# Context rows and key rotations placed behind weight splits, chain buffers turned by one, weight sums three steps later

## The chip, the cores and the metric

The kernel runs on one core of a Trainium2 chip, in fp32 throughout. The metric is the device time of one execution in microseconds. The engines of the core are named as the profile names them: PE (TensorE) multiplies matrices, DVE (VectorE) and ACT (ScalarE) work on elements, POOL (GpSimd) and SP (SyncE) here mostly issue transfers (DMAs). Each engine works through its own instructions in the order in which the program lists them, and waits at an instruction until what that instruction needs is there.

## The reference

One layer of a diffusion block over 512 latent tokens (width 2048) and 256 context tokens. What matters for the change:

```python
shift, scale, gate = jnp.split(silu_c @ w_ada[l] + b_ada[l], 3, axis=-1)
shift_c, scale_c, gate_c = jnp.split(silu_cc @ w_ada[l] + b_ada[l], 3, axis=-1)
h = _modulate(_rmsnorm(xs, norm_g[l]), shift[:, None], scale[:, None])
hc = _modulate(_rmsnorm(cs, norm_g[l]), shift_c, scale_c)
pc_kv = hc @ w_l[:, OFF_K:OFF_ZA]          # keys and values of the context
p = h @ w_l                                # 512 x 2048 times 2048 x 9216
k = _rope(_rmsnorm(_heads(p, OFF_K, N_KV_HEADS), k_norm_g[l]), cos, sin)
...
y_a = (attn * jax.nn.silu(z_a)) @ w_pa
y_b = (_fourier_mix(u_b) * jax.nn.silu(z_b)) @ w_pb
y = (g_a * y_a + g_b * y_b) @ w_o
return _rmsnorm(xs + gate[:, None] * y, final_g)
```

## The kernel before

Every large product is done in fp32 from three reduced-precision matmuls (`mm3`): each operand is split into a high part (`whi`, written by ACT, L176) and the rest (`wlo`, written by DVE, L177), and hi·hi, hi·lo and lo·hi are added in PSUM. Each split of 128x1024 weights thus takes one ACT and one DVE instruction. A *piece* of weights is 128x1024 numbers (512 KB); the 512-token matrix products use it in 12 matmuls of 512 columns.

On top of that stands a Winograd-like scheme with seven products for eight (`PRODUCTS`: P1, Q5, P2, Q6, P7, Q3, Q4). A *group* is one 1024-column block of a weight matrix: seven products of four pieces each, 28 pieces, 336 matmuls. Groups 0 to 7 make the input projection (5, called KV, makes keys and values, and with them the context's, by a second set of matmuls on each piece); then come 48 steps of attention; then groups 10 and 11 (branch projections, three pieces to a product) and groups 8 and 9 (output projection, four pieces).

Four of the seven products use sums of weight blocks that are built up one after the other in the four *chain buffers* `R0` to `R3` (R_1303 to R_1306): a product with `stage` 0 loads its first block into chain buffer `pc` from SP (L215), the later stages add another block to it, by a POOL transfer that accumulates (L280) or by DVE (L259). A chain buffer is loaded for the next group only when its last stage has been split (`left[pc]`). Up to four pieces are split ahead of the one that PE is at (`look`).

Raw weights come through four to six buffers (`raw_pools`), loaded by SP (L212) as soon as a split or an add has read the earlier contents. So DVE's reading sets when SP may issue, and SP issues in the program's order.

Parts that share the engines with the weight splits in the stretch of groups 3 to 5:

- `context_row(i, raw)` (L1070), called four times, forms the seven operand forms of a quarter of the context in one buffer `cparts` (part of the tile `qr`): four weightings on DVE (L1077), a subtraction (L1080), six adds (L1086), four ACT instructions (L1089, L1090), and then a DMA that ACT issues, `cf_d[i]` (L1091). There is only one such buffer, so the weightings of row i+1 wait until the write of row i has landed. Group 5 loads `cf_d` again as pieces `("cf", name)`.
- `load_rotations` (L928; its transfers L929 and L930 are issued by ACT) loads the cos/sin tables and the key gains into the same tile `qr` ahead of group 5, and `rotations` (L935) multiplies them by two DVE instructions. They are used when the first products of keys are done, at the end of P2 of group 5.

In attention, `filler()` fits in the products of the FNet branch (pieces `("pab", j, pc)`, loaded by SP from `in_w_pab`, split by ACT and DVE in order with the softmax work). `weight_sum(n)` (L1410) builds six sums of weight blocks for P7 of groups 10 and 11: a POOL load (L1415), an accumulating POOL load (L1416) and a POOL write to `p7_d` (L1417), at three steps in a row, from step 10 on. Chain buffers 0 to 2 hold gates at that time (`load_gb`, L1216), chain buffer 3 is a scratch tile of `values` (L1315, L1316).

What sets the order: the program is emitted in the order of the code, and a scheduler then moves instructions within each engine by its own estimate of their due times; `tc.issue_after(x)` forces the instructions in its block behind instruction x in that order, without a wait at run time for another engine. `last_split[-1][1]` is the DVE instruction of the weight split that was emitted last, which is up to four pieces ahead of PE.

Of the kernel before, what the change touches and what calls it, by code (L numbers as in the profile page):

```python
# [13 lines left out]
ALU = mybir.AluOpType  # L14
# [76 lines left out]
CHUNKS = (0, 2, 1, 3)  # L91
BRANCH_A, BRANCH_B = 10, (6, 7)
A_CHUNKS = ((0, 2), (1, 3))
A_FORM = {p[0]: (p[1],) for p in PRODUCTS} | {"Q4": ("A12", "A22"), "P2": ()}


# [23 lines left out]
def block_kernel(ctx, tc, xT, ctx_rows, ctx_toks, x, c_row, w_ss, w_gate, vecs, qkg, rope, dft_c, dft_s,  # L120
                 w_start, w_g, w_pab, w_o, final_g, out):
    nc = tc.nc
# [20 lines left out]
    p7_d = dsc.tile([2, 3, P, 1024], F32, name="p7_d")  # L143
# [37 lines left out]
    chain, left = [], [0] * 4  # L181
# [12 lines left out]
    def stream(key, src, *a, **k):  # L194
        todo.append(Piece(key, src if isinstance(src, list) else [src], *a, **k))
# [183 lines left out]
    def stream_product(name, g, w, by_dve, pieces=4):  # L379

        what = next(p[2] for p in PRODUCTS if p[0] == name)
        for pc in range(pieces):
            key = (name, g, pc)
            part = lambda i: w[CHAIN[i][0], CHAIN[i][1], pc]
            if isinstance(what, tuple) and name == "P7" and g >= BRANCH_A:
                stream(key, [p7_d[g - BRANCH_A, pc]], 1024, 2, pc=pc)
            elif isinstance(what, tuple):
                off = name == "P7"
                stream(key, [w[a, b, pc] for a, b in what], 1024, 2, pc=pc, nxt=part(3) if off else None, off=off)
            else:  # L390
                stream(key, [part(what)] if what in by_dve else [], 1024, 2, stage=what, pc=pc,
                       nxt=part(what + 1) if what < (3 if g >= BRANCH_A else 2) and what + 1 not in by_dve else None)
                todo[-1].first = part(0)

# [674 lines left out]

    def context_row(i, raw):  # L1070

        t, raw = cparts, raw.rearrange("p (b s c) -> p b s c", b=4, s=2)
        a11, a21, a12, a22, s3, s2, s4 = (t[:, f] for f in range(7))
        for j in range(2):
            for q in range(2):
                kb = 2 * i + j + 8 * q
                nc.vector.scalar_tensor_tensor(t[:, 2 * q : 2 * q + 2, j, :], raw[:, 2 * q + j], gain[:, kb, 1:2],  # L1077
                                               crs.rearrange("p (s c) -> p s c", s=2), op0=ALU.mult, op1=ALU.mult)

        nc.vector.tensor_tensor(s3, a11, a21, op=ALU.subtract)  # L1080
        for j in range(2):
            sa, sb = (shift[:, 2 * i + j + 8 * q, 1:2] for q in range(2))
            d = sums[:, 6 + j : 7 + j]
            nc.vector.tensor_tensor(d, sa, sb, op=ALU.subtract)
            for o, x, c, y, op in ((s2, a22, sb, s3, ALU.add), (s4, a12, sb, s2, ALU.subtract), (a21, a21, d, a22, ALU.subtract)):
                nc.vector.scalar_tensor_tensor(o[:, j], x[:, j], c, y[:, j], op0=ALU.add, op1=op)  # L1086
        for j in range(2):
            sa, sb = (shift[:, 2 * i + j + 8 * q, 1:2] for q in range(2))
            nc.scalar.activation(a11[:, j], a11[:, j], ACT.Identity, bias=sa)  # L1089
            nc.scalar.activation(t[:, 2:4, j, :], t[:, 2:4, j, :], ACT.Identity, bias=sb)  # L1090
        nc.scalar.dma_start(cf_d[i], t)  # L1091
# [49 lines left out]
    for g, kind in enumerate(KINDS):  # L1141
        if g == 3:
            jobs += [lambda: None] * 12 + [context_norm, lambda: None, lambda: None, context_spread]
        elif g == KV:
            while jobs:
                job()
            assert not any(p[2] == "raw1" for e in ahead for p, _ in e.raws)
        elif g == KV + 1:
            qzs.close()
            gvs, gvp = region("gvp", "right", reuse_waits="tile")  # L1150
            hl_pools += range(MORE_HL)
        group = Group(g, forms, new_ev, {"qz": qz_done, "kv": kv_done, "gate": gate_done}[kind], {"a": "x", "b": "y", "c": "x"})
        if g == KV:
            group.more = Context()
        for name in ONE_GROUP:
            if (g, name) in ((0, "Q4"), (KV + 1, "P1")):
                assert not any(p[2] == "raw0" for e in ahead for p, _ in e.raws)
                load_row(int(g > 0))
            elif (g, name) == (1, "Q5"):
                silu_of_row(0, flat(new_ev()))  # L1160
            if (g, name) == (0, "P7"):
                raw_pools.remove((rp, 1, "raw0", 1))
            if (g, name) == (0, "Q5"):
                hl_pools += range(MORE_HL)
            elif (g, name) == (0, "P2"):

                with tc.issue_after(last_split[-1][1].ins):
                    rotations(HD ** -0.5)
            elif (g, name) == (KV, "P1"):
                load_rotations(qkg[:, 2:4, :])  # L1170
            elif (g, name) == (KV, "Q5"):
                rotations(1.0)
            elif (g, name) == (KV - 1, "Q3"):
                raw_pools.remove((rp, 1, "raw1", 1))
                hl_pools[:] = [p for p in hl_pools if not isinstance(p, int)]
            elif (g, name) == (KV + 1, "Q6"):
                raw_pools += [(rp, 1, "raw1", 1), (gvp, 2, "raw", 2)]
            elif (g, name) == (LAST, "P7"):
                raw_pools.remove((gvp, 2, "raw", 2))
            elif (g, name) == (LAST, "Q3"):  # L1180

                free += [(fms[i], f"s{i}") for i in (4, 5, 6, 7, 12, 13, 14, 15, 8, 9, 10, 11, 2, 3, 0, 1)]
                for h in range(2):
                    load_head(h)
            elif (g, name) == (LAST, "Q4"):
                hl_pools[:] = [p for p in hl_pools if not isinstance(p, int)]
                get_keys(0)
                jobs.append(lambda: turn_queries(0, pair("y")[:, 0, :]))
            group.run(name)
# [16 lines left out]
    assert not any(p[0] is gvp for e in ahead for p, _ in e.raws)  # L1206
    todo_gb, gb = [(j, h) for j in CHUNKS for h in range(2)], {}

    left[:3] = [1] * 3

    def load_gb():
        if todo_gb:
# [212 lines left out]
    for i in range(NSTEP + 3):  # L1425
        h, t = divmod(i, 4)
        if i < NSTEP:
            if t == 2 and h + 2 < NH:
                load_head(h + 2)
            if i % 12 == 10 and i // 12 + 1 < NKV:  # L1430
                get_keys(i // 12 + 1)
            scores(i)
        want = min(3 + 61 * (i + 1) // NSTEP, 64) + (i == NSTEP - 1)
        if want > filled:
            fill(1)
            filled += 1
        if i % 2 == 0 and i >= 4:
            values((i - 4) // 2)
        if 1 <= i <= NSTEP:
            turn(i - 1)  # L1440
            divide(i - 1)
        if t == 1 and h + 1 < NH:
            turn_queries(h + 1, b1())
        if want > filled:
            fill(want - filled)
            filled = want
        if 10 <= i < 28:
            n, step = divmod(i - 10, 3)
            if step == 0:
                weight_sum(n)  # L1450
            else:
                summed[-1][step]()
            if step == 2:
                give(summed.pop()[0])
        if i == 3:
            with tc.issue_after(maxima[0].ins), tc.issue_after(maxima[1].ins):
                e = take((1024,))
                silu_of_row(1, e)
                give(e)
        if i == 33:  # L1460
            for p in more_raw:
                raw_pools.remove(p)
                retired.append(p)
                if not any(r is p for a in ahead for r, _ in a.raws):
                    free.append(p[0::2])
        if i in GATE_STEPS:
            n = NGATE + GATE_STEPS.index(i)
            use_gate(n, get_aside(("gate", n)), maxima[0])
            if n == 2 * KK - 1:
                raw_pools.append((rp, 1, "raw0", 1))  # L1470
        for q, name in {43: [(0, "Z5"), (0, "S3")], 44: [(0, "S2")], 45: [(0, "S4")], 47: [(1, "Z5")], 48: [(1, "S3")],
                        49: [(1, "S2"), (1, "S4")]}.get(i, ()):
            branch_forms(q, name)
        if i == NSTEP - 1:
            a_groups.append(a_group(0))
            first = a_groups[0].steps("P1")
        if NSTEP > i - 2 >= NSTEP - 3:
            next(first)
            next(first)
    ats_.close()  # L1480
    nc.vector.tensor_tensor(gcol, gparts[:, :KK], gparts[:, KK:], op=ALU.add)
    nc.vector.tensor_tensor(gcol, gcol, bada[:, 2 * KK :], op=ALU.add)
    nc.gpsimd.dma_start(gs.rearrange("k p -> p k"), gcol)
# [317 lines left out]
```

## Time and profile before

| what | us |
|---|---|
| timed runs, median of 3 | 1314.68 (1314.44 to 1315.09) |
| the profiled execution, its own time | 1312.46 |
| span of the profiled execution | 1310.7 |
| PE busy in it | 1281.5 |
| DVE busy | 995.5 |
| ACT busy | 685.8 |
| granted TensorE clock (1 is full) | 0.998 |

The page gives busy time, the chain of work that ended last, and the costliest groups; the views of waits show which engine sat idle until which other one was done; the timeline gives single instructions with, in square brackets, the idle time of the engine before them and what ended it. A row "x L328 <- wlo" is a matmul that waited for the low part of its weights. 29 us lie between the span and the busy time of PE.

### The profile page before, as it was taken

The numbers are of one execution on the slowest core, as the hardware profiler recorded it, in microseconds if no ns is written. First come the engines' busy times: TensorE is split into PE (matmuls) and PEld (weight loads), VectorE is DVE, ScalarE is ACT, GpSimd is POOL, SyncE is SP. The second block draws the span as 40 slices with busy tenths as digits, with TensorE's granted clock in tenths as the row PEclk, the third lists the DMA queues.
The fourth block names the chain that finished last, engine by engine and source line by source line (L and its number), as shares of the span: only waits on it lengthen the run. The fifth ranks groups of instructions, "written<-read, shape, count | busy, mean of one in ns | idle before, by whom it ended". The sixth has DMA issues, their size and how long they took to land.

```text
span 1310.7 us, 17551 instructions
## 1 busy us (share of the span) xinstructions
PE 1281.5 (98%) x6522; PEld 1046.7 (80%) x6522; DVE 995.5 (76%) x1295; ACT 685.8 (52%) x1079; POOL 183.3 (14%) x244
## 2 busy tenths in 40 slices
PE   6999999999999999999999999999999999999997
PEld 3577888888888887888888888888888888788885
DVE  5666899989688876757677766688898867787676
ACT  5222655555556544544254554666667646465554
POOL 0110011110202110011021020012100212221210
PEclk9999999999999999999999999999999999999999
DMA  9898487887899979986869888578852899998985
GB/s 381 330 374 349 177 244 188 240 249 244 213 291 263 260 245 276 297 215 175 262 210 285 273 212 260 195 228 264 270 163 81 236 253 246 242 205 231 219 204 171
DMA packets 103718, 318.54 MB, mean 243 GB/s; under 512 B 9808, under 2 KB 33104, under 8 KB 99280
## 3 DMA queue, kind: packets, MB, share of 16 engines
q0 software_dynamic: 30288, 123.75, 39.9%
q1 hardware_dynamic: 48720, 163.65, 35.2%
q10 hardware_dynamic: 24624, 30.02, 6.7%
q8 instruction: 51, 0.84, 0.2%
q14 instruction: 35, 0.29, 0.1%
HBM read 283.30 MB, written 34.09 MB: 242 GB/s over the span
## 4 chain that ended last, share of the span: by engine, by line
PE 73%; DMA 10%; DVE 9%; issue 3%; ACT 3%; SPq 0%; POOL 0%; ACTq 0%; DVEq 0%
PE banks L327 10%; PE banks L328 10%; PE banks L329 9%; PE x L329 6%; PE x L328 6%; PE x L327 6%; PE y L328 5%; PE y L329 5%; PE y L327 5%; DMA wr<-in_w_g 4%; DVE wlo L177 3%; PE pd L532 2%; PE banks L1290 2%; PE pb L327 2%; DVE s L177 2%
## 5 line engine op out<-in xcount | busy, mean ns | idle before, releaser
L176 ACT ACTIVATE whi<-R 128x1024 fp32r<-128x1024 f32 x138 | 145.4, 1060 | 131.6 <-PE banks L329 44.6
L177 DVE TENSOR_TENSOR wlo<-R,whi 128x1024 fp32r<-128x1024 f32 x138 | 167.7, 1222 | 55.3 <-ACT whi L176 53.0
L177 DVE TENSOR_TENSOR wlo<-wr,whi 128x1024 fp32r<-128x1024 f32 (+1 forms) x123 | 148.7, 1214 | 58.8 <-ACT whi L176 58.7
L176 ACT ACTIVATE whi<-wr 128x1024 fp32r<-128x1024 f32 (+1 forms) x123 | 128.9, 1053 | 119.3 <-PE y L329 36.6
L327 PE MATMUL banks<-whi,s 128*128 128x512 f32 x396 | 157.1, 397 | 2.1 <-DVE ev L860 1.5
L328 PE MATMUL banks<-wlo,s 128*128 128x512 f32 x396 | 155.2, 392 | 0.8 <-DVE wlo L177 0.8
L329 PE MATMUL banks<-whi,s 128*128 128x512 f32 x396 | 155.1, 392 | 0.0
L328 PE MATMUL x<-wlo,s 128*128 128x512 f32 x352 | 137.3, 390 | 2.9 <-DVE wlo L177 2.9
L327 PE MATMUL x<-whi,s 128*128 128x512 f32 x352 | 137.2, 390 | 0.0
L329 PE MATMUL x<-whi,s 128*128 128x512 f32 x352 | 137.0, 389 | 0.0
L328 PE MATMUL y<-wlo,s 128*128 128x512 f32 x316 | 123.1, 390 | 0.5 <-DVE wlo L177 0.5
L327 PE MATMUL y<-whi,s 128*128 128x512 f32 x316 | 123.0, 389 | 0.3 <-DVE cxe L1013 0.3
L329 PE MATMUL y<-whi,s 128*128 128x512 f32 x316 | 122.8, 389 | 0.0
L280 POOL DMA_DIRECT2D R<-in_w_g x64 | 56.0, 876 | 423.6 <-DVE wlo L177 241.1
L176 ACT ACTIVATE s<-wr 128x512 fp32r<-128x512 f32 (+2 forms) x93 | 60.7, 677 | 69.2 <-DMA wr<-cf_d 23.7
L327 PEld LDWEIGHTS banks<-whi,s 128*128 128x128 f32 x396 | 74.4, 188 | 17.9 <-ACT whi L176 2.2
L177 DVE TENSOR_TENSOR s<-wr,s 128x512 fp32r<-128x512 f32 (+2 forms) x93 | 67.0, 751 | 27.4 <-ACT s L176 26.6
L329 PEld LDWEIGHTS banks<-whi,s 128*128 128x128 f32 x396 | 74.4, 188 | 15.5
L328 PEld LDWEIGHTS banks<-wlo,s 128*128 128x128 f32 x396 | 74.5, 188 | 15.0 <-DVE wlo L177 1.2
L328 PEld LDWEIGHTS x<-wlo,s 128*128 128x128 f32 x352 | 66.1, 188 | 17.9 <-DVE wlo L177 4.2
L327 PEld LDWEIGHTS x<-whi,s 128*128 128x128 f32 x352 | 66.1, 188 | 13.7
L329 PEld LDWEIGHTS x<-whi,s 128*128 128x128 f32 x352 | 66.1, 188 | 13.6
(293 smaller groups left out, 2835.4 us busy)
## 6 DMA issues: line engine op xcount, KB each, us to landing
wr<-in_w_g SPq DMA_DIRECT2D x128, 512.0 KB, 5.2
R<-in_w_g POOLq DMA_DIRECT2D x64, 512.0 KB, 7.2
wa<-in_w_ss POOLq DMA_DIRECT2D x26, 1024.0 KB, 8.4
R<-in_w_g SPq DMA_DIRECT2D x32, 512.0 KB, 5.7
wr<-in_w_gate SPq DMA_DIRECT2D x32, 512.0 KB, 5.1
wr<-in_w_o SPq DMA_DIRECT2D x24, 512.0 KB, 7.7
R<-in_w_o POOLq DMA_DIRECT2D x24, 512.0 KB, 8.5
wr<-in_w_pab SPq DMA_DIRECT2D x20, 512.0 KB, 6.0
```

Of the source, the lines that this page charges most:

```text
L176: first = nc.scalar.activation(hi, src, ACT.Copy)
L177: return first, nc.vector.tensor_tensor(lo, src, hi.bitcast(F32), op=ALU.subtract)
L280: nc.gpsimd.dma_start(chain[e.pc], e.nxt, accum_op=ALU.add)
L327: nc.tensor.matmul(o, ah, bh, start=start, stop=False, skip_group_check=cont)
L328: nc.tensor.matmul(o, ah, bl, start=False, stop=False, skip_group_check=cont)
L329: nc.tensor.matmul(o, al, bh, start=False, stop=stop, skip_group_check=cont)
L532: last = nc.tensor.matmul(acc[32 * j : 32 * j + 32, :256], c2[:, 8 * h + k, :], w[:, k, :], start=n < 4, stop=n >= KK - 4)
L1290: nc.tensor.transpose(tp[:, k * P : (k + 1) * P], p[:, k * P : (k + 1) * P], ident)
```

## The change

Four edits. (1) The four weightings of each context row are tied behind the DVE half of the weight split that was emitted last. (2) The two rotation instructions for the keys are tied in the same way. (3) Groups 8, 9 and 11 use the chain buffers turned: piece pc of group 11 uses buffer (pc + 3) mod 4, piece pc of groups 8 and 9 buffer (pc + 2) mod 4, where each used buffer pc; buffer 3 now counts as taken until attention is over. (4) The weight sums start at step 13 in place of step 10.

```diff
+CHAIN_FROM = {BRANCH_A + 1: 3, 8: 2, 9: 2}
...
             part = lambda i: w[CHAIN[i][0], CHAIN[i][1], pc]
+            r = (pc + CHAIN_FROM.get(g, 0)) % 4
             if isinstance(what, tuple) and name == "P7" and g >= BRANCH_A:
-                stream(key, [p7_d[g - BRANCH_A, pc]], 1024, 2, pc=pc)
+                stream(key, [p7_d[g - BRANCH_A, pc]], 1024, 2, pc=r)
             elif isinstance(what, tuple):
                 off = name == "P7"
-                stream(key, [w[a, b, pc] for a, b in what], 1024, 2, pc=pc, nxt=part(3) if off else None, off=off)
+                stream(key, [w[a, b, pc] for a, b in what], 1024, 2, pc=r, nxt=part(3) if off else None, off=off)
             else:
-                stream(key, [part(what)] if what in by_dve else [], 1024, 2, stage=what, pc=pc,
+                stream(key, [part(what)] if what in by_dve else [], 1024, 2, stage=what, pc=r,
...
     def context_row(i, raw):
 
-        t, raw = cparts, raw.rearrange("p (b s c) -> p b s c", b=4, s=2)
+        t, raw, line = cparts, raw.rearrange("p (b s c) -> p b s c", b=4, s=2), last_split[-1][1].ins
...
-                nc.vector.scalar_tensor_tensor(t[:, 2 * q : 2 * q + 2, j, :], raw[:, 2 * q + j], gain[:, kb, 1:2],
-                                               crs.rearrange("p (s c) -> p s c", s=2), op0=ALU.mult, op1=ALU.mult)
+                with tc.issue_after(line):
+                    nc.vector.scalar_tensor_tensor(t[:, 2 * q : 2 * q + 2, j, :], raw[:, 2 * q + j], gain[:, kb, 1:2],
+                                                   crs.rearrange("p (s c) -> p s c", s=2), op0=ALU.mult, op1=ALU.mult)
...
             elif (g, name) == (KV, "Q5"):
-                rotations(1.0)
+                with tc.issue_after(last_split[-1][1].ins):
+                    rotations(1.0)
...
-    left[:3] = [1] * 3
+    left[:] = [1] * 4
...
-        if 10 <= i < 28:
-            n, step = divmod(i - 10, 3)
+        if 13 <= i < 31:
+            n, step = divmod(i - 13, 3)
...
     ats_.close()
+    left[3] = 0
```

## The prediction

> **What bounds the kernel now.** I read the page's span and busy times first.
>
> ```profile
> span 1310.7 us, 17551 instructions
> ...
> PE 1281.5 (98%) x6522; PEld 1046.7 (80%) x6522; DVE 995.5 (76%) x1295; ACT 685.8 (52%) x1079; POOL 183.3 (14%) x244
> ```
>
> The span is 1310.7 us and PE is busy for 1281.5 of them, so 29.2 us is all that any reordering can win, and no engine but PE is near its limit. The order of PE's own instructions is the same in both programs, so what can change is only how long PE idles. Second view: whom PE waited for (total, times, longest, in us).
>
> ```profile
> PE pd L495 <- DVE s L494: 8.7, 1, 8.7
> PE x L328 <- DVE wlo L177: 2.9, 3, 2.1
> PE banks L327 <- DVE ev L860: 1.5, 1, 1.5
> PE banks L1129 <- DVE ptl L177: 0.8, 1, 0.8
> PE banks L328 <- DVE wlo L177: 0.8, 1, 0.8
> PE y L328 <- DVE wlo L177: 0.5, 1, 0.5
> ```
>
> The 8.7 us are at the start. The others are small: low halves of weight splits (`wlo`) that came late, 2.9 + 0.8 + 0.5; a wait of 1.5 for the last sums of the input projection; 0.8 in attention for `ptl`. Third view: the span in stretches (busy us of PE, PEld, DVE, ACT, POOL with instruction counts, then granted clock, DMA share, GB/s).
>
> ```profile
> 0.00:33.00 33.00, 22.36 (x122) 11.63 (x122) 16.40 (x35) 18.14 (x32) 3.17 (x13) 1.00 0.95 381
> ...
> 396.00:429.00 33.00, 33.00 (x147) 27.32 (x147) 29.81 (x37) 20.35 (x40) 8.18 (x8) 1.00 0.94 250
> ...
> 475.40:555.80 80.40, 77.14 (x337) 62.74 (x336) 60.86 (x81) 38.32 (x51) 6.90 (x8) 1.00 0.87 263
> ...
> 1287.00:1320.00 33.00, 14.19 (x62) 11.26 (x60) 12.44 (x28) 11.25 (x29) 0.00 (x0) 0.90 0.36 131
> ```
>
> The first 33 us hold 33.00 - 22.36 = 10.6 us of idle, the last stretch 1310.7 - 1287 - 14.19 = 9.5: start and tail, which the change leaves alone. Of the 9 us between them 80.40 - 77.14 = 3.26 lie in group 4 (475.4 to 555.8), where the last two of the four context rows are worked on. At 396 to 429 PE has no idle at all. The third view so says where to look: group 4, the step from group 11 to group 8, and attention. Fourth view, PE's timeline at two of the three stalls of group 4:
>
> ```profile
> 505.09 0.39 PE L329 MATMUL x<-whi,s 128*128 128x512 f32 x1
> 505.32 0.39 PE L327 MATMUL x<-whi,s 128*128 128x512 f32 x1
> 506.33 0.50 PE L328 MATMUL x<-wlo,s 128*128 128x512 f32 x1 [0.62 <-DVE wlo L177]
> 506.67 0.40 PE L329 MATMUL x<-whi,s 128*128 128x512 f32 x1
> ...
> 522.38 0.50 PE L328 MATMUL x<-wlo,s 128*128 128x512 f32 x1 [2.13 <-DVE wlo L177]
> ```
>
> Undisturbed, one matmul follows the other by 505.32 - 505.09 = 0.23. Across the first stall the steps are 1.01 and 0.34, together 0.89 more than two of 0.23, for an idle time of 0.62: I add 0.27 to every stall's idle time for the restart.
>
> **The change part by part.** *Context rows.* DVE in the same stretch, with what it waited for, and PE at the matmul that needs the split:
>
> ```profile
> 473.76 0.48 DVE L1077 SCALAR_TENSOR_TENSOR qr<-wr,gain,qr 128x256 f32<-128x256 f32 x1 [5.28 <-DMA cf_d<-qr]
> 474.16 1.22 DVE L177 TENSOR_TENSOR wlo<-R,whi 128x1024 fp32r<-128x1024 f32 x1
> ...
> 475.63 0.39 PE L328 MATMUL x<-wlo,s 128*128 128x512 f32 x1
> ...
> DVE qr L1077 <- DMA cf_d<-qr: 13.3, 3, 6.5
> ```
>
> The weightings of a row (L1077) wait for the previous row's write out of `qr`, 13.3 us in three waits, and everything behind them on DVE waits too. At 473.76, for the third row, this was 5.28; the split behind it ended at 475.38 and PE took it at 475.63, so the lead of four pieces was used up to 0.25 us. The adds into the chain buffers (L259), also behind, are what frees the raw weight buffers, so SP's loads stopped. The busy tenths of the DMA engines, 40 slices of 1 us from 470 to 510, show it:
>
> ```profile
> DMA  9995000267003889969999999999999999999999
> ```
>
> DMA runs empty around 474 to 481 and is then full up to the end. In the chain of waits (start, duration):
>
> ```profile
> 489.40 0.41 DVE qr L1077
> ...
> 489.82 14.05 DMA wr<-in_w_g
> ...
> 511.69 3.55 DMA cf_d<-qr
> ...
> 515.72 4.05 DMA qr<-in_qkg
> ...
> 528.24 9.61 DMA wr<-cf_d
> ```
>
> The load issued at 489.82, released by a weighting, took 14.05 us, and its split came late: the stall at 506.33. In the changed order of DVE already the second row's weightings stand behind five more splits (the one of 474.16 is the last of them) and one subtraction of products, and an add into `R` precedes the row's six adds; the third and fourth row move alike. No weighting then stands ahead of a split that PE is about to need, and the previous write has five splits' time, over 5 us, to land. What DVE has to do stays the same:
>
> ```profile
> L1077 DVE SCALAR_TENSOR_TENSOR qr<-wr,gain,qr x16: 477/481/485, 449.4 to 506.8; 128x256 f32<-128x256 f32 x16
> L1086 DVE SCALAR_TENSOR_TENSOR qr<-qr,shift x16: 343/348/352, 452.0 to 510.5; 128x128 f32<-128x128 f32 x16
> ...
> L935 DVE SCALAR_TENSOR_TENSOR qr<-qr x2: 686/690/693, 519.9 to 520.5; 128x512 f32<-128x512 f32 x2
> ...
> DMA to landing us min/median/max: 3.5/5.1/10.3
> ```
>
> Four weightings of 0.481 and six adds of 0.348 are 4.0 us per row, now in one run; four pieces of lead, 4 x 12 x 0.23 = 11 us, cover it, and if the lead were 0.25 as now it would cost up to 4.0 each time. The load that took 14.05 is asked for earlier by up to the 5.28: between nothing (the 0.89 stay) and all (0.89 gone). I take all, since the empty slices alone hold some 5 us of transfers. The order of SP changes in this stretch too: one raw load that waited for the second row's buffer now stands behind three chain loads, which so start earlier.
>
> *Rotations.* The two instructions wait for their tables, and later a context piece comes late to ACT:
>
> ```profile
> 519.89 1.29 DVE L935 SCALAR_TENSOR_TENSOR qr<-qr 128x512 f32<-128x512 f32 x2 [2.04 <-DMA qr<-in_qkg]
> ...
> 537.96 1.16 ACT L176 ACTIVATE s<-wr 128x512 fp32r<-128x512 f32 x2 [6.71 <-DMA wr<-cf_d]
> ```
>
> DVE stood 2.04 for the gains (loaded 515.72, 4.05 us) and then spent 2 x 0.69 on the product, ahead of the split that PE awaited at 522.38 for 2.13. Behind 32 later rows, where the tables have long landed, both cost nothing: the lead hides 1.4 us. ACT issues the table loads and blocks until the last row's write has landed (3.5 to 10.3 us); they stand behind four half splits now, behind two whole ones before, so the block stays about as long. The last stall, 0.51 at 542.24, is the split behind the first context piece (load issued 528.24, 9.61 us, ACT waited 6.71). That load was queued behind the splits that the two waits held up; it comes earlier with them. Together: 0.62 + 2.13 + 0.51 + 3 x 0.27 = 4.1 us, at least 2.13 + 0.27 = 2.4 if only the rotations' share goes.
>
> *Chain buffers.* The first piece of group 8 waits for its chain load, and PE for its split:
>
> ```profile
> 1134.83 8.02 DMA R<-in_w_o
> ...
> 1145.33 0.50 PE L328 MATMUL banks<-wlo,s 128*128 128x512 f32 x1 [0.75 <-DVE wlo L177]
> ```
>
> The load could be issued only when the last stage of group 11 had left buffer 0. Turned, this piece uses buffer 2, which group 11 (buffers 3, 0, 1) does not touch, so its load stands some ten places earlier on SP; the second piece then has the issue time of today's first (1134.83, landing 1142.85) and is needed 12 x 0.23 = 2.8 us later than it. That is 0.75 + 0.27 = 1.0 us gained; none if the second piece turns late instead. DVE, ACT and PE keep their orders from here to the end.
>
> *Weight sums.* POOL's first sum, the load beside it, and what waited:
>
> ```profile
> 847.14 0.53 POOL L1415 DMA_DIRECT2D s<-in_w_pab  x1 [4.21 <-ACT s L176]
> ...
> 858.97 6.09 DMA wr<-in_w_pab
> ...
> 865.14 1.06 ACT L176 ACTIVATE whi<-wr 128x1024 fp32r<-128x1024 f32 x1 [1.62 <-DMA wr<-in_w_pab]
> ...
> 868.83 0.44 PE L1129 MATMUL banks<-ident,wr 128*128 128x128 f32 x2 [0.78 <-DVE ptl L177]
> ...
> wr<-in_w_pab SPq DMA_DIRECT2D x20, 512.0 KB, 6.0
> ```
>
> ACT stood 1.62 for a load of 6.09 us, and PE 0.78 at 868.83. But the loads of this kind land in 6.0 at the median, so this one was not slowed by the sums, and moving them frees little. Bounds: the stall goes (0.78 + 0.27 = 1.1 gained), or the sum's read now falls beside this load and ACT waits another 1.62. I take nothing. No load of their results stands near them in SP's order.
>
> The sum is -4.1 - 1.0 + 0 = -5.1 us. The profiled execution took 1312.46 (span and 1.8 around it); it becomes 1307.4. The runs shown have a median of 1314.68, 2.2 above the profiled one, so the timed median becomes 1309.6.
>
> **The rivals.** (a) *The rotations alone.* The write and load times in the queue stay as they are and only 2.4 goes, with the 1.0 of the chain: -3.4, 1311.3. For it: 14.05 and 9.61 are times of a full queue. (b) *DMA bounds the stage.* Its share is 0.87 over group 4; what DVE gains is then waited for in the next late load and only the 1.0 stays: 1313.7. Against it: 396 to 429 has 0.94 and no idle. (c) *Sums beside loads.* The six sums now fall among other loads for the filler, and ACT's 1.62 is paid three times more: +4.9 - 5.1, 1314.5. The Trainium skill (DMA: Bandwidth & Descriptors, Queues, rings and completion order) says that each DMA engine takes turns between the queues that have work, packet by packet, so that POOL's sum would slow SP's load even where SP issued first; the 6.0 at the median says that it matters little. (d) *The row in one run, slower.* If the first chain loads of group 4 are not earlier, the lead at 475.6 stays 0.25, and the second row's 4.0 and an add of 1.22 stand right ahead of the next split, 1.22 more: PE, which needs it 2.8 later, idles 4.0 + 1.22 + 1.22 - 2.8 = 3.6; the third row does the same. 7.2 + 2 x 0.27, less 2.4 and 1.0: +4.3, 1319.0. It decides where the split that ended at 475.38 does not end before some 471. Against it: the wait of 5.28 lies right ahead of that split and goes. (e) The edit may not do what it says only where the order ignored it; the built order shows all four moved.
>
> **How the numbers follow.** Forecast 0.60, (a) 0.13, (b) 0.11, (c) 0.07, (d) 0.09. The forecast alone spans 1308.5 (the 1.1 of attention gained as well) to 1311.2 (1.62 lost). For 8 in 10 the range must take in (a) and (b), not (d), and some room below for restarts dearer than 0.27: 1307.0 to 1313.7. Within 0.2% (2.6 us, about what a measurement can tell) are (b) and (c) with some of (a)'s neighbourhood: 0.17; faster 0.73; slower 0.10.
>
> **What the profile will show.** Right: DVE's wait on `cf_d` near zero where 13.3 stood, no DVE wait on `in_qkg`, DMA tenths without the empty stretch at 474 to 481, no PE stall for `wlo` in group 4, PE idle of group 4 under 0.5; no wait on `wlo` at the first piece of group 8. Wrong: (a) a late raw load or context piece on ACT with a stall of 0.5 or more; (b) the same idle under other names; (c) more ACT waits on `in_w_pab`; (d) PE waiting 3 us or more near 478. A tail or start longer than 9.5 and 10.6 would be none of these.

## The result and the profile after

| what | us |
|---|---|
| kernel before, median of 6 runs | 1314.56 (1310.37 to 1315.09) |
| kernel after, median of 6 runs | 1306.12 (1305.52 to 1309.5) |
| ratio, with 95% interval | 0.9944 (0.9928 to 0.996) |
| profiled execution of after, its own time | 1305.55 (before 1312.46) |

The change makes the kernel 8.4 us faster by the medians (5.3 to 9.5 by the interval), 6.9 by the two profiled executions' own times and 7.4 by their spans. The forecast was 5.1. The measured 1306.12 lies 3.5 below the predicted 1309.6 and 0.9 below the low end of the range.

The page of after, its span and busy times:

```profile
span 1303.3 us, 17544 instructions
...
PE 1279.5 (98%) x6522; PEld 1047.4 (80%) x6522; DVE 995.1 (76%) x1295; ACT 685.4 (53%) x1079; POOL 180.6 (14%) x244
```

The work is the same (DVE 995.1 against 995.5), and PE's idle time falls from 29.2 to 23.8 us. Whom PE waited for in after (total, times, longest), answering to the second view of the prediction; all lines have moved down by one to four:

```profile
PE pd L497 <- DVE s L496: 8.5, 1, 8.5
PE banks L328 <- DVE ev L862: 1.5, 1, 1.5
...
PE y L329 <- DVE wlo L178: 0.3, 1, 0.3
```

The three waits of `x` for `wlo`, the one of `banks` for `wlo` (first piece of group 8) and the one of L1129 for `ptl` in attention are gone. The 8.5 at the start and the 1.5 ahead of attention stand. In stretches, with the columns as in the prediction:

```profile
0.00:33.00 33.00, 22.47 (x124) 11.84 (x124) 16.60 (x36) 18.75 (x33) 3.16 (x13) 1.00 0.95 383
474.53:551.33 76.80, 76.52 (x337) 62.96 (x336) 56.70 (x79) 39.23 (x51) 6.88 (x8) 1.00 0.91 277
1287.00:1320.00 33.00, 7.27 (x32) 5.59 (x30) 8.26 (x19) 8.83 (x23) 0.00 (x0) 0.89 0.34 128
```

The second row is group 4, from the same matmul to the same matmul as 475.40 to 555.80 in before: 76.80 us in place of 80.40, with 0.28 idle in place of 3.26. The first row still has 10.5 us of idle; after the last one's start there are 1303.3 - 1287 - 7.27 = 9.0.

DVE's list of waits in after has no row for `cf_d` (13.3 us in before) and none for `in_qkg` (2.04). The busy tenths of the DMA engines in the 40 us that answer to 470 to 510 of before:

```profile
DMA  4797999367879599999999999999999999700285
```

The run of near-empty slices (before: `5000267003`) has become single dips. At the very end of the row are new empty slices. SP waited there, up to its next load at 505.87, for a raw buffer that the fourth context row still had to read on DVE (view of SP's waits from 500 to 530):

```profile
SPq L213 <- DVE qr L1083: 7.3, 1, 7.3
```

In before, SP's waits for context rows from 465 to 510 were 2.1 and 0.9. No stall of PE followed the longer one.

PE issues the same matmuls in the same order in both kernels, so the start of each in one trace can be subtracted from its start in the other, and the difference changes only where time is won or lost. From before to after it goes: -0.87 when the first group begins and still -0.87 at the start of group 4; -4.47 at its end; -4.32 ahead of 679 and -5.1 behind 692, in two steps (PE idled there once in before, 0.19 at 679.38); -5.9 behind 868.83; -6.9 behind the first piece of group 8 and up to the last matmuls. (The span is another 0.5 shorter behind these, but 2.2 us of the execution lie outside it in place of 1.8, so the own times differ by 6.9, as the matmuls do.) So the places that the change touches gave 3.6 (group 4) and 1.2 (group 8), 4.8 together, near the forecast. The other 2.1 of the 6.9 stand where the forecast had nothing: 0.9 at the start, 0.8 near 680 to 692 and 0.9 at 868.83, less some 0.4 lost elsewhere. The experiments had to tell whether the edits won those too.

### The profile page after: what moved, and what is told of

It reads as the page before. It is cut to its first block, busy times and chain, and to the rows that moved or that the text cites. A ratio compares the mean times of both kernels' runs of the same rounds, so it can differ in the third digit from the quotient of the medians.

```text
span 1303.3 us, 17544 instructions
## 1 busy us (share of the span) xinstructions
PE 1279.5 (98%) x6522; PEld 1047.4 (80%) x6522; DVE 995.1 (76%) x1295; ACT 685.4 (53%) x1079; POOL 180.6 (14%) x244
## 4 chain that ended last, share of the span: by engine, by line
PE 91%; DMA 3%; DVE 2%; ACT 2%; issue 1%; SPq 0%; ACTq 0%; DVEq 0%
PE banks L328 10%; PE banks L329 10%; PE banks L330 10%; PE x L328 9%; PE x L330 9%; PE x L329 9%; PE y L329 7%; PE y L328 7%; PE y L330 7%; PE pd L534 2%; PE banks L1294 2%; PE pb L328 2%; PE pb L330 2%; PE pb L329 2%; DMA wa<-in_w_ss 1%; PE pc L328 1%
```

## The experiments

All are compared with the kernel before, run beside them. "Group 4" is its length, from the start of one matmul to the start of another, the same two in every kernel; without any wait it takes 76.16.

| kernel | median, us | ratio (95%) | group 4, us |
|---|---|---|---|
| before, four executions of its order there | | | 80.40, 82.15, 81.35, 82.31 |
| rotations alone | 1312.36 | 0.9988 (0.9976 to 1.0) | 81.16 |
| context rows alone | 1308.81 | 0.9958 (0.9946 to 0.9971) | 78.50 |
| chain buffers alone | 1310.92 | 0.9983 (0.9973 to 0.9992) | (81.35) |
| weight sums alone | 1313.77 | 1.0003 (0.9992 to 1.0015) | (82.31) |
| rows and rotations | 1307.59 | 0.9963 (0.9951 to 0.9976) | 76.59 |
| after without the sums | 1305.45 | 0.9947 (0.9934 to 0.9959) | 76.65 |
| rotations alone, tables later | 1309.23 | 0.9976 (0.9966 to 0.9987) | 77.60 |
| after, tables later | 1305.61 | 0.9948 (0.9934 to 0.9961) | 76.16 |
| after again | 1306.39 | 0.9946 (0.9926 to 0.9965) | 76.18 |
| after, tables later, again | 1305.68 | 0.9944 (0.9923 to 0.9965) | 76.16 |

The chain buffers and the sums do not touch group 4, so their lengths (in brackets) are two of the four of before. Before had medians of 1313.64, 1312.36 and 1313.64 in these three sets.

### The rotations alone

```diff
             elif (g, name) == (KV, "Q5"):
-                rotations(1.0)
+                with tc.issue_after(last_split[-1][1].ins):
+                    rotations(1.0)
```

> The kernel before with the two rotation instructions alone tied behind the weight split (context rows, chain buffers and weight sums as before). Theory of the prediction: the stall of 2.13 us of group 4 (matmul that waited for the low half, 522.38 in the trace of before) goes, the one of 0.62 at 506.33 stays, the one of 0.51 at 542.24 may stay: the idle of PE between 475.4 and 555.8 falls from 3.26 to 0.6 to 1.2 us, and the time by 2.4 to 3.2 us. Rival, DMA bounds the stage: the wait turns into another one of about the same length in the stage and the time falls by less than 0.5 us.

The time fell by 1.3 us (0 to 3.2). PE's timeline in this kernel, around the two stalls at the end of group 4, and the load of the first context piece:

```profile
539.95 0.50 PE L327 MATMUL y<-whi,s 128*128 128x512 f32 x1 [0.96 <-ACT whi L176]
542.08 0.50 PE L328 MATMUL y<-wlo,s 128*128 128x512 f32 x1 [1.63 <-DVE wlo L177]
...
525.31 0.39 SPq L212 DMA_DIRECT2D wr<-cf_d  x1
...
537.80 1.15 ACT L176 ACTIVATE s<-wr 128x512 fp32r<-128x512 f32 x2 [4.34 <-DMA wr<-cf_d]
```

The stall of 2.13 is gone, and 0.96 + 1.63 stand where 0.51 stood. The piece was asked for 2.9 us earlier (525.31 against 528.24) and was there no earlier: ACT took it at 537.80, against 537.96 in before. PE was 2.5 us earlier, and so waited longer for the same load. What the DMA engines did meanwhile (last two numbers: their busy share and GB/s):

```profile
520.00:540.00 20.00, 19.04 (x85) 15.44 (x83) 12.74 (x15) 7.46 (x10) 1.73 (x2) 1.00 1.00 272
```

They were busy all the time. Group 4 takes 81.16, against the 80.40 of the profile on which the forecast was made. Of that, 0.9 was lost at its second matmul, long before the rotations:

```profile
475.42 0.50 PE L328 MATMUL x<-wlo,s 128*128 128x512 f32 x1 [0.55 <-DVE wlo L177]
```

It is the split that the prediction found with a lead of 0.25. It ended when it did in before (475.4), behind the third row's weighting, but PE was there 0.92 us earlier in this execution. Without this stall the group takes 80.3, as before: the whole gain is given back one load later. (Against all four executions of before, 81.6 on average, it is 0.4 shorter; the timing says 1.3; the last section says what the longer ones lost.) So the 2.4 of rival (a) is refuted, and the mechanism of rival (b) seen, for this edit by itself.

### The context rows alone

The tie of the weightings, nothing else:

```diff
+        t, raw, line = cparts, raw.rearrange("p (b s c) -> p b s c", b=4, s=2), last_split[-1][1].ins
...
-                nc.vector.scalar_tensor_tensor(t[:, 2 * q : 2 * q + 2, j, :], raw[:, 2 * q + j], gain[:, kb, 1:2],
...
+                with tc.issue_after(line):
+                    nc.vector.scalar_tensor_tensor(t[:, 2 * q : 2 * q + 2, j, :], raw[:, 2 * q + j], gain[:, kb, 1:2],
...
```

> The kernel before with the weightings of the context rows alone tied behind the weight split. Theory of the prediction: DVE's waits for cf_d (13.3 us in before) fall to near zero, the stall of 0.62 goes and the one of 2.13 for the rotations stays: idle of group 4 falls from 3.26 to 2.1 to 2.6 us, the time by 0.9 to 1.7 us. Rival, the rows set all of it: with the rows' transfers out of the way the gains land in time, the 2.13 goes too and the time falls by over 3 us. Rival, the row in one run is slower: a stall of 3 us or more near 478 and a time 3 to 7 us longer.

4.8 us faster (3.8 to 7.1), far more than the theory gave; the rival that the rows set all of it had said over 3. In the profile group 4 is 1.9 us shorter than in the first one of before and 3.1 shorter than in the four on average; the rest of the 4.8 is not placed. What the DMA engines moved from 460 to 500 in before, with the rotations alone, with the rows alone, and in after, four views of four kernels in this order:

```profile
DMA packets 2600, 10.19 MB, mean 255 GB/s; under 512 B 263, under 2 KB 263, under 8 KB 2598
```

```profile
DMA packets 2563, 10.06 MB, mean 251 GB/s; under 512 B 260, under 2 KB 260, under 8 KB 2561
```

```profile
DMA packets 2927, 11.47 MB, mean 287 GB/s; under 512 B 311, under 2 KB 311, under 8 KB 2925
```

```profile
DMA packets 2959, 11.61 MB, mean 290 GB/s; under 512 B 322, under 2 KB 322, under 8 KB 2957
```

The rows move some 1.3 MB into these 40 us, which at 287 GB/s is 4.5 us of transfers; the rotations move none. Both the 0.62 and the 2.13 are gone; what is left of the stage's stalls, on PE, and DVE's wait for the gains:

```profile
540.25 0.50 PE L328 MATMUL y<-wlo,s 128*128 128x512 f32 x1 [1.99 <-DVE wlo L177]
```

```profile
530.97 0.69 DVE L935 SCALAR_TENSOR_TENSOR qr<-qr 128x512 f32<-128x512 f32 x1 [1.11 <-DMA qr<-in_qkg]
```

One thing clouds this run: in the built order the rotations have moved too, fourteen and fifteen DVE instructions back, because the scheduler estimates anew. So the rows do not take the 2.13 quite by themselves. That part was not told apart: a tie can push an instruction back, but not hold it forward.

### Rows and rotations together

The two edits above in one kernel.

> The kernel before with the weightings of the context rows and the rotations both tied, chain buffers and weight sums as before. Theory of the prediction: together they take the whole stall of group 4 (3.26 us idle, 4.1 with restarts), stalls for the low half at 506, 522 and 542 all gone or under 0.5 us, and the time is 3.5 to 5 us below before. Rival, from the run with the rows alone (4.8 us faster): the rows do it all, and with the rotations tied too the time is within 0.5 us of that run.

```profile
475.42:552.01 76.59, 76.50 (x337) 62.95 (x336) 57.70 (x80) 39.28 (x52) 6.88 (x8) 1.00 0.92 283
```

Group 4 has 0.09 us of idle left, the time is 4.8 us lower (3.1 to 6.4). By time this is what the rows alone gave; by group 4 it is 1.9 better than they. The intervals of the two are too wide to tell 1.9 us, so by the time the rival stands. The traces show where the last stall went. With the rows alone, the second rotation still ran between the splits behind the context piece, and held them up by 0.6; ACT also took the piece 1.2 us later than here. (The profile names PE as what ended that wait of ACT; the longest load of a context piece in this kernel, 13.4 us, would end there too, since the first was asked for at 521.84.) The rows alone first, then rows and rotations:

```profile
535.37 1.16 ACT L176 ACTIVATE s<-wr 128x512 fp32r<-128x512 f32 x2 [6.31 <-PE y L329]
...
536.65 0.68 DVE L935 SCALAR_TENSOR_TENSOR qr<-qr 128x512 f32<-128x512 f32 x1
```

```profile
534.18 1.15 ACT L176 ACTIVATE s<-wr 128x512 fp32r<-128x512 f32 x2 [5.63 <-DMA wr<-cf_d]
```

The 0.6 is the tie's; whether the 1.2 is too, one execution of each cannot say.

### Do transfers beside the context piece make it late?

The tables of the rotations, loaded by ACT, 640 KB, go behind the first context piece; once with the rotations alone, once in after:

```diff
-            elif (g, name) == (KV, "P1"):
-                load_rotations(qkg[:, 2:4, :])
             elif (g, name) == (KV, "Q5"):
+                with tc.issue_after(last_split[-1][0].ins):
+                    load_rotations(qkg[:, 2:4, :])
+            elif (g, name) == (KV, "P2"):
                 with tc.issue_after(last_split[-1][1].ins):
                     rotations(1.0)
```

> The kernel before with the rotations alone tied, and the load of their tables (128x1024 and 128x256 numbers, 640 KB) issued some 45 us later, behind the first context piece. With the rotations alone tied, the 2.13 us went and the stalls at that piece grew from 0.51 to 0.96 + 1.63. Theory: the piece lands late because the DMA engines are full from 482 on (about 270 GB/s); with 640 KB less ahead of it, about 2.4 us of transfers, it lands some 2 us earlier and the stalls fall from 2.6 to under 1 us. Rival: its landing hangs on the time when it is issued (525.3), not on what runs beside it; the stalls stay at 2 to 2.6 us.

> The kernel after with the load of the rotations' tables issued some 45 us later, behind the first context piece, and the two rotations six DVE instructions later. If transfers beside the context piece make it late: its last stall (0.28 us at 537.77 in after) goes, the piece lands 1 to 2 us earlier, and the time falls by 0 to 0.6 us. If not: the time is that of after; if the tables are now late for the keys: a wait of DVE for them near 575 and a time longer by 1 us or more.

With the rotations alone:

```profile
539.80 0.50 PE L328 MATMUL y<-wlo,s 128*128 128x512 f32 x1 [0.98 <-DVE wlo L177]
...
524.53 0.39 SPq L212 DMA_DIRECT2D wr<-cf_d  x1
...
535.52 1.15 ACT L176 ACTIVATE s<-wr 128x512 fp32r<-128x512 f32 x2 [4.52 <-DMA wr<-cf_d]
```

The piece was asked for 0.8 us earlier than with the rotations alone and reached ACT 2.3 us earlier; the stalls fell from 2.6 to 0.98. The chain of waits gives the load's own time: with the rotations alone, with the tables later, and with rows and rotations tied:

```profile
525.31 12.39 DMA wr<-cf_d
```

```profile
524.53 10.88 DMA wr<-cf_d
```

```profile
521.53 12.55 DMA wr<-cf_d
```

With 640 KB less beside it the load took 1.5 us less, so what runs beside it does make it late, as far as one execution of each can show. With the rows tied it is as slow as ever, 12.55, but it is asked for 3.8 us earlier than with the rotations alone, while PE is only 0.9 earlier: there the piece is in time because of its issue. (The stall of 0.61 at 506 was missing in this execution, although nothing ahead of it had changed; I can't say why.) In after the same edit leaves no idle in group 4 at all:

```profile
475.02:551.18 76.16, 76.16 (x338) 63.07 (x336) 57.39 (x80) 39.47 (x51) 6.88 (x8) 1.00 0.91 276
```

But in its second execution after itself had none either (76.18), and the times agree (below).

### The chain buffers alone

```diff
+CHAIN_FROM = {BRANCH_A + 1: 3, 8: 2, 9: 2}
...
+            r = (pc + CHAIN_FROM.get(g, 0)) % 4
...
-    left[:3] = [1] * 3
+    left[:] = [1] * 4
...
     ats_.close()
+    left[3] = 0
```

> The kernel before with the chain buffers of groups 8, 9 and 11 turned, nothing else. Theory of the prediction: the stall of 0.75 us at the first piece of group 8 (1145.33 in before) goes and with it 1.0 us of the time; nothing else changes. Rival, the second piece turns late instead: a stall of some 0.7 us for a low half 2 to 4 us later, and no change of the time.

2.7 us faster by the medians; the interval is 1.1 to 3.5. Before, in its second execution, and this kernel, at the first piece of group 8:

```profile
1145.00 0.49 PE L327 MATMUL banks<-whi,s 128*128 128x512 f32 x1 [0.26 <-ACT whi L176]
1146.26 0.49 PE L328 MATMUL banks<-wlo,s 128*128 128x512 f32 x1 [0.77 <-DVE wlo L177]
```

```profile
1143.22 0.48 PE L328 MATMUL banks<-whi,s 128*128 128x512 f32 x1
1143.54 0.40 PE L329 MATMUL banks<-wlo,s 128*128 128x512 f32 x1
1143.77 0.39 PE L330 MATMUL banks<-whi,s 128*128 128x512 f32 x1
```

Both stalls go, and no later one comes: matmul against matmul, this kernel wins 1.4 us there against the second execution of before and 1.2 against the first, and after wins 1.2 against the first. The rest of the 2.7 has no place in the trace.

### The weight sums, alone and taken out

This edit alone; and after with these two lines as they were:

```diff
-        if 10 <= i < 28:
-            n, step = divmod(i - 10, 3)
+        if 13 <= i < 31:
+            n, step = divmod(i - 13, 3)
```

> The kernel before with the weight sums at steps 13 to 30 in place of 10 to 27, nothing else; only POOL's order changes. Theory of the prediction: nothing, the stall of 0.78 us in attention (868.83 in before) stays and the time is within 0.5 us of before. Rival 1, from the trace after, where this stall is gone: the first sum beside the load of 6.09 us made that load late, and without it the stall goes, 0.8 to 1.1 us less. Rival 2, the sums now fall beside other loads for the filler: new waits of ACT for in_w_pab of over 1.5 us each, and a time longer by 1 to 5 us.

> The kernel after with the weight sums back at steps 10 to 27, all else as after. Theory of the prediction and of the run with the sums alone: the sums are worth nothing, the time is that of after within 0.5 us (8 us below before), and the stall of 0.78 us in attention (868.83 in before), which was missing in all four single edits as well, does not come back. Rival: beside the other edits the sums are worth some 1 us; the stall comes back and the time is 7 us below before.

Alone they change the time by +0.1 us (-1.1 to +2.0), and after without them is 6.9 us faster than before (5.4 to 8.7), at 1305.45, beside 1305.61 for the version with the sums and the tables later in the same set. In neither run does the stall of 868.83 appear.

### Before and after once more

> The kernel before once more, unchanged, for a second profile of it. Theory: the stalls of 0.78 us at 868.83 and of 0.19 at 679.38 are missing, as in the single edits that do not touch these stretches, the stalls of group 4 sum to 3.3 to 4.5 us of idle time, and the one of 0.75 at the first piece of group 8 stands. Rival: the two small stalls are there again, so the edits took them away.

> The kernel after once more, unchanged. The predicted gain was 5.1 us, the first runs of after gave 8.4 by the medians and 7.4 by the spans of two executions. Theory: 1.2 of the 2.0 us beyond it at the stalls near 679 and 869 and 0.9 at the start were the execution of before that was profiled, not the edits; the gain over more runs is 6 to 7.5 us (ties 4.6, chain buffers 1.4). Rival: the edits are worth 8 us or more together, over the sum of the single ones.

> The kernel after with the tables' load later, as in the run before of the same kernel, beside the kernel after on one chip. It had no idle time at all in group 4, where after had 0.28 in one execution. Theory: 0.3 to 0.6 us faster than after, which is within what the timing can tell; rival: the same or slower, since the two differ by executions more than by this.

Before in its second execution ran the products behind 868.83 without that stall:

```profile
868.75 0.28 PE L329 MATMUL banks<-pth,s 128*128 128x256 f32 x1
868.90 0.44 PE L1129 MATMUL banks<-ident,wr 128*128 128x128 f32 x2
```

Against the first profile of before, every other execution, the second of before included, gains 0.9 us there, and 0.6 to 0.8 near 680 to 692. Those 1.7 us in the comparison of the two profiles were thus the execution, not the edits. So is the start: when the first group begins, the other executions are between 0.92 earlier and 0.03 later than the first profile, before's second one 0.76 earlier.

After again is 7.25 us below before (4.6 to 9.7). It lost 1.97 once in attention, a wait for a gate's sum:

```profile
916.17 0.50 PE L328 MATMUL banks<-whi,s 128*128 128x512 f32 x1 [1.97 <-DVE R L1242]
```

This wait was 0.25 in the first execution of after and 0.74 in the second of before, so it belongs to no edit either. The version with the tables later is 0.7 us below after on the same chip, within what the runs can tell; I would not call it better.

## Why the prediction was right, and where it was too small

**The bound.** Right in the main: of the 7.4 us of span, 5.4 are idle time of PE, and the stages named (group 4, group 8) are where the edits moved it. The other 2.0 are busy time of the same matmuls (1281.5 to 1279.5), 0.6 of it in group 4 (77.14 to 76.52): the steps stretched behind a stall, for which the forecast added 0.27 each, count as busy.

**Context rows.** The mechanism is shown: no wait for `cf_d`, no empty stretch, 1.3 MB more before 500, 0.62 and its restart gone. The size was too small: they were taken at 0.89 and were worth 1.9 to 3.1 in group 4 by themselves. The 2.13 went with them, in part by the order that the scheduler then chose, and the context piece was asked for at 521.84 in place of 528.24. Rival (d), the row in one run, did not show: no stall near 478 in any kernel with the rows tied.

**Rotations.** That the 2.13 would go was right. That this was worth 2.4 by itself, "if only the rotations' share goes", was the wrong step: alone it was worth nothing in group 4 against the profile that the forecast went by (80.3 without the stall at the group's start, 81.16 with it, against 80.40), because the context piece, asked for 2.9 us earlier, took 12.39 us in place of 9.61 and landed no earlier. I had charged the 0.51 to the splits that the two waits held up; the runs show it charged to the transfers beside the piece (1.5 us for 640 KB of them), and what outran them was the earlier issue that came with the rows. The 0.51 went to 0.28 or to nothing only with both.

**The size of group 4.** Forecast 4.1. The profiled pair has 3.6. Over the executions, before takes (80.40 + 82.15 + 81.35 + 82.31) / 4 = 81.6, the four with both ties and the tables where they were (76.80, 76.59, 76.65, 76.18) 76.6: 5.0 us. The one profile of before that I had was its best of four. In the two worst, PE's clock fell as well (last section).

**Chain buffers.** Right in place and mechanism; 1.2 to 1.4 in place of 1.0, since the high half also came up to 0.26 late.

**Weight sums.** Nothing, as taken. The 0.78 that was the bound of a gain was chance, and rival (c) did not show: ACT waited for `in_w_pab` for 5.4 us in before, 6.2 with the sums alone, 1.6 and 5.2 in two executions of after.

**From the profiled time to the median.** I added the 2.2 by which before's median exceeds its profiled time, as if after would keep it. It did not: after's median is 0.6 above its profiled time. Part of that 2.2 may be the very stalls that went: group 4 was 0.9 to 1.9 us longer in the other three executions of its order. With the terms from the traces, 5.0 + 1.4 = 6.4, within the interval of 5.3 to 9.5; the 2.0 us from there to 8.4, or 0.8 to the 7.25 of the second comparison, are not placed.

## What to carry to other kernels

A stall that is taken away is only won if the next thing that PE needs is earlier too: look whether its transfer is late by its issue or by a full queue, and if the queue is full, look upstream for the stretch where it ran empty. One profile gives one draw of each stall; where a stall hangs on transfers, take its size from several executions before it goes into a sum, and don't add an unexplained offset to what is left.

## What the hardware showed beyond this

A stall can cost more than its idle time. In before's second execution PE waited 2.94 us for the low half, and was slow afterwards. The matmuls, and the stretches (PE's busy time with its count first, the granted clock third from the end):

```profile
520.07 0.39 PE L327 MATMUL x<-whi,s 128*128 128x512 f32 x1
523.39 0.60 PE L328 MATMUL x<-wlo,s 128*128 128x512 f32 x1 [2.94 <-DVE wlo L177]
523.80 0.63 PE L329 MATMUL x<-whi,s 128*128 128x512 f32 x1
524.22 0.63 PE L327 MATMUL x<-whi,s 128*128 128x512 f32 x1
...
527.14 0.39 PE L328 MATMUL x<-wlo,s 128*128 128x512 f32 x1
```

```profile
524.00:528.00 4.00, 4.00 (x12) 3.17 (x12) 4.00 (x5) 2.23 (x4) 1.51 (x2) 0.62 1.00 287
528.00:532.00 4.00, 4.00 (x19) 3.30 (x19) 4.00 (x5) 3.04 (x4) 0.21 (x1) 1.00 1.06 245
```

From 523.39 to 527.14 there are nine steps between matmuls, 0.42 each in place of 0.23: 1.7 us on top of the 2.94. Over single microseconds the granted clock was 0.50. With the weight sums alone the same stall was 2.58, and the clock fell too, but 1.5 us after PE had resumed at 523.77. One row of before's second execution, then three with the weight sums alone:

```profile
524.00:525.00 1.00, 1.00 (x3) 0.79 (x3) 1.00 (x2) 0.00 (x0) 0.00 (x0) 0.50 0.97 193
```

```profile
524.00:525.00 1.00, 1.00 (x5) 0.81 (x5) 1.00 (x3) 0.00 (x0) 0.00 (x0) 1.00 1.10 213
525.00:526.00 1.00, 1.00 (x4) 0.81 (x4) 1.00 (x2) 0.00 (x0) 0.00 (x0) 0.62 1.02 205
526.00:527.00 1.00, 1.00 (x4) 0.71 (x4) 1.00 (x2) 0.85 (x2) 0.42 (x1) 0.50 1.04 225
```

With the chain buffers alone it was 2.37, and in the first profile of before 2.13, both without a drop:

```profile
522.05 0.50 PE L329 MATMUL x<-wlo,s 128*128 128x512 f32 x1 [2.37 <-DVE wlo L178]
522.39 0.40 PE L330 MATMUL x<-whi,s 128*128 128x512 f32 x1
522.63 0.40 PE L328 MATMUL x<-whi,s 128*128 128x512 f32 x1
```

Against the same matmuls at undisturbed steps of 0.227, this stall cost 2.4 us in the first profile of before, 2.7 with the chain buffers alone, but 4.5 and 4.8 in the two executions where the clock fell: its idle time and 0.3 in the former, its idle time and 1.9 in the latter. Between 2.37 and 2.58 us of idle the price jumped, in these four; where exactly, and whether it is always there, was not tried. The Trainium skill (TensorE: Matmul & The Clock Gate, What's actually happening) says that PE's clock is halved after an idle window of some 3.4 us, on windows that run freely. The granted clock of 0.50 and the slow steps of 0.42 against 0.23 agree with the half rate; the idle time that was enough was shorter than that window here, 2.58 (2.97 from the start of one matmul to the start of the next).
